# The first residual of two chunks by plain loads and VectorE additions; the sigmoid product and the state copies planned anew

## The chip, the cores and the metric

The kernel runs on one core of a Trainium2 chip. The metric is the device time of one execution in microseconds; several runs are given with their median. The engines are called TensorE (PE in the profile, PEld for its weight loads), VectorE (DVE), ScalarE (ACT), GpSimd (POOL) and SyncE (SP, which here only issues DMAs).

## What is computed

One layer of a hybrid decoder for 1024 prompt tokens and 8 sequences of 4 sample tokens, in f32, with 1024 features:

```python
h = _rmsnorm(x, g_pre_mix[l]) * (1.0 + sc1) + sh1
z = h @ w_in[l]
za, zq, zf, zi, zg, zc = jnp.split(z, split_at, axis=-1)
ya, v_rows = _chunk_gmlp(za, ...)          # gMLP, chunks of 128
yb, S = _hgrn2(zq, zf, zi, zg, ...)        # gated linear recurrence
yc, buf = _conformer_conv(zc, ...)         # depthwise convolution, layer norm, silu
y = jnp.concatenate([ya, yb, yc], axis=-1) @ w_out[l]
x = x + gt1 * _rmsnorm(y, g_post_mix[l])   # first residual
h = _rmsnorm(x, g_pre_mlp[l]) * (1.0 + sc2) + sh2
y = jnp.square(jax.nn.relu(h @ w_up[l])) @ w_down[l]
x = x + gt2 * _rmsnorm(y, g_post_mlp[l])   # second residual
```

`_conformer_conv` ends with `silu(_layernorm(y))`, that is a product of a value and its sigmoid. `_hgrn2` needs the recurrent state at the start of each block of tokens.

## The kernel before

Features lie on the partitions. The 1056 tokens are cut into three chunks (`NCH`) of 352 (`CW`); the sample tokens are the last 32 of chunk 2. A tile of 1024 features by 352 tokens is 8 slices of 128 features; where it is kept in three tiles (`KK`), these hold 3, 3 and 2 slices, that is 1056, 1056 and 704 elements per partition. Each f32 product is made of three matmuls of rounded high and low parts, so each weight block of 128 by 1024 is split after its load: a cast on ScalarE (`whi`), a subtraction on VectorE (`wlo`). `fetch` (line 304) issues the loads on SyncE's queue into three buffers (`raw`), `weights` (line 344) keeps a small stock of split blocks ready.

**Order.** The program is written in the order in which each engine shall run it. A main program issues the matmuls; all else is done by generators in queues (line 216), which `step` (line 224) lets go on between the pieces of a product, as far as the credits of the engines allow. A generator can wait for planned times: `until` (line 244) yields until the class `Plan` (line 39) holds the given tiles for done. `Plan` knows for each engine when it will be free, by formulas for the price of every instruction: on ScalarE 0.1 us and 0.83 ns per element and 1.3 us for a change of table, for a DMA on GpSimd's queue 0.9 us and 8.0 us until it has landed. These times set only the order in which instructions are issued; on the chip semaphores do the waiting, and each engine takes its instructions in the order issued.

**Mixer.** `ORDER` names the blocks of the input projection: two for the convolution, four pairs of the recurrence with their gates, and the gMLP. A product's result stands in one of three PSUM banks (`pm_tile`) until it is evacuated; for a gate that takes a sigmoid on ScalarE (`sgg`) and a product on VectorE (`gq`). `conv_tail` (line 931) normalises the convolution's output and ends, for both halves j, with an affine step in place and a sigmoid on ScalarE and their product on VectorE, issued one behind the other. `recur` (line 1197) makes the recurrence of one pair of heads: the states S, one per block of 64 tokens, are copied by two ScalarE instructions, with dimensions swapped, into `sv[0]` (the tile `vt`, in the profile under the name vf) and `sv[1]` (in `KE`, in the profile K); `until(vt, KE, k2, QE, banks=2)` stands ahead of the matmuls `ob`, which read them.

**Out-projection and first residual.** The y tiles of the mixer are split into `yh` and `yl` by `split_y` for each chunk. For each of the chunks 0, 1, 2 eight blocks m of the output projection follow (line 1519 on); ScalarE evacuates each into `o` and its square for a sum (`tot`). Blocks 6 and 7 keep their split weights for all chunks (the tiles whome). Behind the last block a generator `after_mix` (line 1495) is queued: the root mean square from `tot` (`stps`, `rstd`), the scaling of `o` on VectorE, three DMAs on GpSimd's queue that add x from memory onto `o`, three more that write the sum to memory as `x1d` for the second residual, then squares (ScalarE), their fold (VectorE), a matmul of ones (`stps<-sq`), and the normalisation and modulation in place, which gives the high and low parts of h2 (`h20hi`, `h20lo` for chunk 0 and so on).

**MLP.** TensorE then makes four up-projections for chunk 0, four for chunk 1, eight blocks of down-projection for both, and the same for chunk 2; each first waits, in the program, until that chunk's h2 has been issued. Twelve further rounds follow, in which TensorE has hardly a gap.

The tiles tagged "e" (line 186 on) share 17 buffers (`N_E`): the y tiles, `o` of chunks 0 and 1, the kept weights, later the activations of the MLP. `load3` (line 609) takes three such tiles and loads a chunk of x into them on SyncE's queue.

Of the kernel before, what the change touches and what calls it, by code (L numbers as in the profile page):

```python
# [11 lines left out]
ALU = mybir.AluOpType  # L12
# [14 lines left out]
T_GROUP = 3.57  # L27
# [11 lines left out]
class Plan:  # L39
# [10 lines left out]
    def given(self, key, price, out, ins, extra=0.15):  # L50
        names = [x.tensor.name for x in ins]
        end = max(self.free[key], self.now(), *(self.done.get(x, 0.0) for x in names)) + price
        self.free[key] = end
        out = out.tensor.name
        self.done[out] = end + extra
        for x in (out, *names):
            self.used[x] = max(self.used.get(x, 0.0), end)
        self.moved |= key == "pe"

    def idle(self, t):  # L60

        if not self.moved:
            self.free["pe"] += t
        self.moved = False
# [95 lines left out]
def trunk_kernel(ctx: ExitStack, tc: tile.TileContext, xT, cT, wada0, wada, vec, cst, msk, win, wout, wup,  # L160
# [4 lines left out]
    plan = Plan()  # L165
    PE = Metered(nc.tensor, pe_price, credit, "pe", plan)
    ACT = Metered(nc.scalar, ActPrice(), credit, "act", plan)
    DVE = Metered(nc.vector, dve_price, credit, "dve", plan)
    POOL = Metered(nc.gpsimd, pool_price, credit, "pool", plan)
# [34 lines left out]
    def e3(name):  # L204
        return ep.tile([128, 3, CW], F32, tag="e", name=name)
# [15 lines left out]
    def add_task(kind, gen):  # L221
        queues[kind].append(gen)

    def step(t):

        plan.idle(t)
        t += max(0.0, clock[1] - credit["pe"])
        clock[0] += t
        for k in ("dve", "act", "pool"):
            credit[k] = min(credit[k] + t, t + 0.5)  # L230
        credit["pe"] = clock[1] = min(credit["pe"] + t, 1.0)
        again = True
        while again:
            again = False
            for kind, q in queues.items():
                if q and due[kind] <= clock[0] and all(credit[k] > 0 for k in uses.get(kind, ("dve", "act", "pe"))):
                    try:
                        due[kind] = clock[0] + (next(q[0]) or 0.0)
                    except StopIteration:
                        q.pop(0)  # L240
                    again = True
                    break

    def until(*aps, banks=0):

        while not plan.ready(aps, banks):
            yield 0.2
# [23 lines left out]
    def vc(o, n):  # L271
        return vec_t[:, o:o + n]
# [259 lines left out]
    def add_last(tot):  # L532
        DVE.tensor_tensor(out=tot, in0=tot, in1=pending.pop(), op=ALU.add)
# [72 lines left out]
    def hc(name):  # L606
        return hp.tile([128, 8, CW], F32, tag="c", name=name)

    def load3(src, name):
        ts = []  # L610
        for kk, (k0, n) in enumerate(KK):
            t = e3(f"{name}{kk}")
            SP.dma_start(out=t[:, 0:n, :], in_=src[:, k0:k0 + n, :])
            ts.append(t)
        return lambda kk: ts[kk][:, 0:KK[kk][1], :]
# [233 lines left out]
    ysp = [None] * NCH  # L849

    def split_y(c):
        hi, lo = hc(f"yh{c}"), hc(f"yl{c}")
        for k in Y_ORDER:
            while y_done[k] <= c:
                yield 0.5
            y = ch(ys[k], c)
            ACT.copy(out=r(hi[:, k, :]), in_=y)
            DVE.tensor_tensor(out=r(lo[:, k, :]), in0=y, in1=hi[:, k, :], op=ALU.subtract)
            yield
        ysp[c] = lambda k: (hi[:, k, :], lo[:, k, :])  # L860
# [70 lines left out]
    def conv_tail():  # L931
        while not room(3):
            yield 2.0
        sq, hi, lo = [e("y6")], e("cvhi"), e("cvlo")
        for c in range(NCH):
            DVE.tensor_tensor(out=ch(sq[0], c), in0=ch(cva[0], c), in1=ch(cva[1], c), op=ALU.add)
        yield 4.0

        def halves():
            ACT.copy(out=r(hi), in_=sq[0])  # L940
            POOL.tensor_tensor(out=r(lo), in0=sq[0], in1=hi, op=ALU.subtract)

        halves()
        yield from until(hi, lo)
        for c in range(NCH):
            yield from until(banks=1)
            mu = pb.tile([128, CW], F32, tag="b", name="cmu")
            mean_of(mu, mean256, ch(hi, c), ch(lo, c))
            s2 = rs("sq2")[:, 0:CW]
            for j in range(2):  # L950
                DVE.tensor_tensor(out=ch(cva[j], c), in0=ch(cva[j], c), in1=mu, op=ALU.subtract)
                ACT.activation(out=s2 if j else ch(sq[0], c), in_=ch(cva[j], c), func=AF.Square)
            DVE.tensor_tensor(out=ch(sq[0], c), in0=ch(sq[0], c), in1=s2, op=ALU.add)
            yield
        yield 4.0
        halves()
        yield from until(hi, lo, banks=3)
        vv = [pb.tile([128, CW], F32, tag="b", name="cvv") for c in range(NCH)]
        for c in range(NCH):
            mean_of(vv[c], mean256, ch(hi, c), ch(lo, c))  # L960
        drop(2)
        sq.append(e("y7"))
        for c in range(NCH):
            ACT.activation(out=ch(sq[0], c), in_=vv[c], func=AF.Sqrt, bias=eps, scale=1.0)
        yield 2.0
        for c in range(NCH):
            sd = ch(sq[0], c)
            DVE.reciprocal(out=sd, in_=sd)
            yield
            for j in range(2):  # L970
                a = ch(cva[j], c)
                DVE.tensor_tensor(out=a, in0=a, in1=sd, op=ALU.mult)
            yield
        yield 2.0
        for j in range(2):
            z = cva[j]
            ACT.activation(out=z, in_=z, func=AF.Identity, scale=vc(V_LNG + j, 1), bias=vc(V_LNB + j, 1))
            yield
            ACT.activation(out=sq[j], in_=z, func=AF.Sigmoid)
            DVE.tensor_tensor(out=sq[j], in0=sq[j], in1=z, op=ALU.mult)  # L980
            ys[6 + j] = sq[j]
            y_done[6 + j] = NCH
            drop()
            yield
# [212 lines left out]
    def recur(p, st):  # L1197
# [59 lines left out]
        sv = vt, by_block(KE)  # L1257
# [3 lines left out]
        for i in range(2):  # L1261
# [5 lines left out]
                 in_=D64.rearrange("p (o b) -> p o b", o=1).to_broadcast([128, 32, 16]))  # L1267
# [4 lines left out]
        for hh in range(2):  # L1272
            o = 64 * hh
            ACT.copy(out=sv[hh][o:o + 64, 1:16], in_=S[o:o + 64, :, 0:15].rearrange("p d b -> p b d"))
        ACT.copy(out=hg_o[:, p, :], in_=S[:, :, 15])

        yield from until(vt, KE, k2, QE, banks=2)
# [10 lines left out]
        oo, sq, hi, lo = k2, vf, e("gnhi"), e("gnlo")  # L1288
# [19 lines left out]
        for hh in range(2):  # L1308
# [7 lines left out]
                           op=ALU.mult)  # L1316
# [175 lines left out]
    def extra(name):  # L1492
        return e2.tile([128, 3, CW], F32, tag="e2", name=name)

    def after_mix(c, src, tot):
        box = []
        yield 1.0
        yield from until(tot, banks=1)
        rstd = rstd_of(tot)
        yield  # L1500
        for kk in (normed(c, src, rstd, Go1) if c == 2 else scaled(c, src, rstd, ())):
            k0, n = KK[kk]
            POOL.dma_start(out=src(kk), in_=xT[c][:, k0:k0 + n, :], accum_op=ALU.add)
            yield
        for kk, (k0, n) in enumerate(KK):
            POOL.dma_start(out=x1d[c, :, k0:k0 + n, :], in_=src(kk))
        yield from until(*(src(kk) for kk in range(3)))
        for d in sum_squares(src, box):
            yield d
        hi, lo = hc(f"h2{c}hi"), hc(f"h2{c}lo")  # L1510
        for d in modulated(c, src, box.pop(), G2, sh2, hi, lo):
            yield d
        h2[c] = (hi, lo)
# [5 lines left out]
    for c in range(NCH):  # L1519
        src, o = blocks_of([(e3 if c < 2 else extra)(f"o{c}") for kk in KK])  # L1520
        tot = w2.tile([128, CW], F32, tag="tot", name="tot", bufs=2)
        while ysp[c] is None:
            step(T_GROUP / 2)
        for m in range(8):
            w = w_kept[m] if m in w_kept else weights()
            if m in KEPT:
                w_kept[m] = w
            ps = pm_tile()
            product8(ps, w, ysp[c], Y_ORDER)
            if c == 2 and m in (2, 3, 4, 5, 6):  # L1530
                split_next()
            if c < 2:
                ACT.activation(out=o(m), in_=ps, func=AF.Identity, scale=Go1[:, m, 0:1])
            else:
                ACT.copy(out=o(m), in_=ps)
            add_square(tot, ps, m, DVE)
            step(T_GROUP / STEPS)
            if c == 0 and m in (1, 3):
                add_task("first", split_y(1 + m // 2))
        add_last(tot)  # L1540
        add_task(("recur", "turn", "stage")[c], after_mix(c, src, tot))


    acc = [None] * NCH
# [423 lines left out]
    acts, more = {}, {}  # L1968
# [12 lines left out]
    for g, parts in enumerate(GROUPS):  # L1981
        tot = tots[:, 2 * g:2 * g + 2, :].rearrange("p a n -> p (a n)")[:, 0:sum(b - a for c, a, b in parts)]
# [113 lines left out]
```

## Time and profile before

| | us |
|---|---|
| runs | 1258.51, 1260.38, 1264.3 |
| median | 1260.38 |
| the profiled execution | 1263.86 |
| its span, first to last instruction | 1262.1 |
| its mean granted clock of TensorE | 0.990 |

The span is what the profile's times count in; the execution's own time has 1.8 us around it. In the profile nearly all instructions bear line 113, the helper that records them, so they are told apart by the names of their tiles: `a<-b,c` is an instruction that writes a and reads b and c. In a group's row stand the instruction, its shape, the count, then the busy time and the mean of one, then the idle time of the engine ahead of it and what ended that. In a row of a timeline stand start, duration, engine, line, operation, and in brackets the engine's idle time ahead of it with what ended it.

### The profile page before, as it was taken

To read this page: it belongs to the slowest core of one execution; us is meant where nothing else is said; L and a number is where in the kernel's file an instruction comes from. 1 tells how busy PE (TensorE), PEld (TensorE's weight loads), DVE (VectorE), ACT (ScalarE), POOL (GpSimd) and SP (SyncE) were. 2 spreads that over 40 slices of the span, in tenths; PEclk is the share of its full clock that TensorE was granted. 3 is DMA by queue.
4 is the path that set the end of the run, shared out by engine and by line. 5 is a ranking of instruction groups with operands and counts; after the bars stand their busy time and mean duration, and the time that the engine had idled before them with its cause. 6 is when DMAs were issued, how large, how long until landed. Compare 5 with 4: busy or idle time off the path is not lost.

```text
span 1262.1 us, 20853 instructions
## 1 busy us (share of the span) xinstructions
PE 1221.9 (97%) x8614; PEld 1171.4 (93%) x8614; DVE 902.0 (71%) x1469; ACT 533.6 (42%) x989; POOL 63.0 (5%) x107
## 2 busy tenths in 40 slices
PE   9999999999899999999999999999999999999995
PEld 7888889999889999899999999999999999999994
DVE  5799889688658768866686657657666765765766
ACT  6513464684854746555423312322331331231533
POOL 1000020211010011000000000000000000000001
PEclk9999999999999999999999999999999999999998
DMA  9458401111111466243201211210211120111218
GB/s 367 170 217 277 168 26 52 43 59 47 35 43 40 151 192 182 85 134 106 79 18 50 68 34 34 68 49 19 68 50 34 51 68 32 36 67 35 108 18 210
DMA packets 48846, 113.22 MB, mean 90 GB/s; under 512 B 10336, under 2 KB 24832, under 8 KB 48624
## 3 DMA queue, kind: packets, MB, share of 16 engines
q1 hardware_dynamic: 44432, 99.22, 22.9%
q0 software_dynamic: 4320, 12.68, 4.3%
q8 instruction: 67, 1.10, 0.4%
q14 instruction: 27, 0.22, 0.1%
HBM read 101.75 MB, written 10.14 MB: 89 GB/s over the span
## 4 chain that ended last, share of the span: by engine, by line
PE 78%; DVE 11%; ACT 6%; DMA 3%; issue 2%; POOL 0%; SPq 0%; DVEq 0%; ACTq 0%
PE pmt L113 71%; DVE acc L113 2%; PE adaps L113 1%; DMA rawada<-in_wada 1%; DVE T L113 1%; PE pmt L744 1%; DVE wlo L113 1%; DMA o<-in_xT 1%; ACT K L113 1%; ACT vf L113 1%; DVE q L113 1%; PE sc L113 1%; DVE rsq L113 1%; ACT relu L113 1%; PE ob L113 1%
## 5 line engine op out<-in xcount | busy, mean ns | idle before, releaser
L113 PE MATMUL pmt<-ah,whi 128*128 128x352 f32 (+2 forms) x744 | 244.0, 328 | 7.9 <-DVE acc L113 5.8
L113 PE MATMUL pmt<-al,whi 128*128 128x352 f32 (+2 forms) x744 | 241.3, 324 | 1.3 <-DVE al L113 1.3
L113 PE MATMUL pmt<-ah,wlo 128*128 128x352 f32 (+2 forms) x744 | 240.1, 323 | 0.0
L113 DVE TENSOR_TENSOR acc<-acc,pmt 128x352 f32<-128x352 f32 (+1 forms) x320 | 158.5, 510 | 91.8 <-PE pmt L113 91.6
L113 DVE TENSOR_TENSOR wlo<-raw,whi 128x1024 fp32r<-128x1024 f32 (+2 forms) x113 | 134.5, 1192 | 46.2 <-ACT whi L113 46.2
L113 ACT CAST whi<-raw 128x1024 fp32r<-128x1024 f32 (+2 forms) x113 | 114.2, 1014 | 107.9 <-PE pmt L113 105.8
L113 PEld LDWEIGHTS pmt<-ah,whi 128*128 128x128 f32 x744 | 139.7, 188 | 15.3 <-DVE acc L113 10.7
L113 PEld LDWEIGHTS pmt<-al,whi 128*128 128x128 f32 x744 | 139.9, 188 | 4.2 <-DVE al L113 2.0
L113 PEld LDWEIGHTS pmt<-ah,wlo 128*128 128x128 f32 x744 | 139.9, 188 | 0.4
L113 ACT COPY acc<-pmt 128x352 f32<-128x352 f32 x63 | 28.4, 452 | 196.7 <-PE pmt L113 161.8
L113 PE MATMUL pmt<-h22hi,wlo 128*128 128x352 f32 x256 | 82.7, 323 | 0.0
L113 PE MATMUL pmt<-h22hi,whi 128*128 128x352 f32 x256 | 82.5, 322 | 0.0
L113 PE MATMUL pmt<-h22lo,whi 128*128 128x352 f32 x256 | 82.3, 322 | 0.0
L113 DVE SCALAR_TENSOR_TENSOR cva<-cvx,vec_t,cva 128x1024 f32<-128x1024 f32 x60 | 77.7, 1295 | 1.2
L113 PE MATMUL pmt<-s,whi 128*128 128x352 f32 x312 | 75.6, 324 | 0.0
L113 ACT ACTIVATE relu<-pmt 128x352 f32<-128x352 f32 x57 | 26.4, 463 | 104.2 <-PE pmt L113 101.3
L113 DVE TENSOR_TENSOR al<-rsq,ah 128x352 fp32r<-128x352 f32 x96 | 49.1, 523 | 15.7 <-ACT ah L113 9.6
L113 PE MATMUL pmt<-h1hi,whi 128*128 128x352 f32 x168 | 55.7, 332 | 2.6 <-DVE gq L113 2.6
L113 PE MATMUL pmt<-h2hi,whi 128*128 128x352 f32 x168 | 56.7, 337 | 0.0
L113 PE MATMUL pmt<-h0hi,whi 128*128 128x352 f32 x168 | 55.5, 330 | 0.8 <-DVE gq L113 0.8
L113 PEld LDWEIGHTS pmt<-s,whi 128*128 128x128 f32 x312 | 54.5, 188 | 0.0
L113 DVE TENSOR_TENSOR rsq<-relu 128x352 f32<-128x352 f32 x45 | 23.5, 523 | 43.0 <-ACT relu L113 41.8
(391 smaller groups left out, 2941.0 us busy)
## 6 DMA issues: line engine op xcount, KB each, us to landing
rawada<-in_wada SPq DMA_DIRECT2D x48, 512.0 KB, 8.3
raw<-in_wup SPq DMA_DIRECT2D x36, 512.0 KB, 3.5
raw<-in_wdn SPq DMA_DIRECT2D x48, 256.0 KB, 3.1
raw<-in_win SPq DMA_DIRECT2D x22, 512.0 KB, 3.6
raw<-in_wout SPq DMA_DIRECT2D x20, 512.0 KB, 3.5
raw<-in_wdn SPq DMA_DIRECT2D x12, 512.0 KB, 3.5
x<-in_xT SPq DMA_DIRECT2D x6, 528.0 KB, 7.0
o<-in_xT POOLq DMA_DIRECT2D x6, 528.0 KB, 7.8
```

The costliest lines, as they stand in the source:

```text
L113: return f(**kw)
L744: nc.tensor.matmul(out=pss[m, c], lhsT=r(w_first[m][i % 2][:, k, :]), rhs=r(h[c][i // 2][:, k, :]), start=k == i == 0, stop=k == 7 and i == 2)
```

## The change

1. `Plan.more` is new: it lengthens the planned work of an engine and the planned end of tiles, without any instruction.
2. In `conv_tail` the affine step counts for 0.9 us more, and the product of sigmoid and value is issued only when the plan holds the sigmoid for done; the second half's activations are issued behind the first half's product.
3. In `recur` each of the two state copies counts for 0.95 us more.
4. For chunks 0 and 1, behind block 6 of the out-projection, x is loaded again into three tiles of SyncE's queue, once the y parts of chunks 1 and 2 have been issued. `after_mix` adds these tiles to `o` on VectorE, straight behind each scaling, in place of the accumulating DMAs.
5. Chunk 2 keeps its accumulating DMAs and gets a pause of 4.0 us of the plan's clock behind the writes of x1.

```diff
+    def more(self, key, t, *outs):
+        self.free[key] += t
+        for x in outs:
+            x = x.tensor.name
+            self.done[x] = max(self.done[x], self.free[key] + 0.15)
+            self.used[x] = max(self.used[x], self.free[key])
...
             ACT.activation(out=z, in_=z, func=AF.Identity, scale=vc(V_LNG + j, 1), bias=vc(V_LNB + j, 1))
+            plan.more("act", 0.9, z)
             yield
             ACT.activation(out=sq[j], in_=z, func=AF.Sigmoid)
+            yield from until(sq[j])
             DVE.tensor_tensor(out=sq[j], in0=sq[j], in1=z, op=ALU.mult)
...
             ACT.copy(out=sv[hh][o:o + 64, 1:16], in_=S[o:o + 64, :, 0:15].rearrange("p d b -> p b d"))
+            plan.more("act", 0.95, sv[hh])
...
-    def after_mix(c, src, tot):
+    def after_mix(c, src, tot, x):
...
-            POOL.dma_start(out=src(kk), in_=xT[c][:, k0:k0 + n, :], accum_op=ALU.add)
+            if x:
+                DVE.tensor_tensor(out=src(kk), in0=src(kk), in1=x(kk), op=ALU.add)
+            else:
+                POOL.dma_start(out=src(kk), in_=xT[c][:, k0:k0 + n, :], accum_op=ALU.add)
             yield
         for kk, (k0, n) in enumerate(KK):
             POOL.dma_start(out=x1d[c, :, k0:k0 + n, :], in_=src(kk))
+        if not x:
+            yield 4.0
...
+        x_again = None
...
+            if c < 2 and m == 6:
+                while not (ysp[1] and ysp[2]):
+                    step(T_GROUP / 2)
+                x_again = load3(xT[c], f"xa{c}_")
         add_last(tot)
-        add_task(("recur", "turn", "stage")[c], after_mix(c, src, tot))
+        add_task(("recur", "turn", "stage")[c], after_mix(c, src, tot, x_again))
```

## The prediction

> **What bounds the kernel now.** I read the page first, then who waited for whom on TensorE, then TensorE's timeline at the longest of these waits, then stretches of 3.4 us around them.
>
> ```profile
> span 1262.1 us, 20853 instructions
> PE 1221.9 (97%) x8614; PEld 1171.4 (93%) x8614; DVE 902.0 (71%) x1469; ACT 533.6 (42%) x989; POOL 63.0 (5%) x107
> PE 78%; DVE 11%; ACT 6%; DMA 3%; issue 2%; POOL 0%; SPq 0%; DVEq 0%; ACTq 0%
> ```
>
> TensorE is busy for 1221.9 of 1262.1 us. The change takes no matmul away, so it can only win from the 40.2 us in which TensorE is idle and from time at a lower clock. Which of these gaps does it touch? The waits of TensorE name them:
>
> ```profile
> PE pmt L113 <- DVE gq L113: 3.5, 2, 2.6
> PE ob L113 <- ACT K L113: 3.2, 4, 1.5
> PE pmt L113 <- DVE h21lo L113: 2.4, 1, 2.4
> PE stps L113 <- DVE sq L113: 2.2, 1, 2.2
> PE ob L113 <- ACT vf L113: 0.5, 1, 0.5
> 329.68 0.43 PE L113 MATMUL pmt<-h1hi,whi 128*128 128x352 f32 x1 [2.63 <-DVE gq L113]
> 354.50 0.27 PE L113 MATMUL ob<-QB,K 128*64 128x64 f32 x1 [1.52 <-ACT K L113]
> 468.22 1.54 PE L113 MATMUL stps<-sq,cst_t 128*128 128x352 f32 x2 [2.22 <-DVE sq L113]
> 527.90 0.43 PE L113 MATMUL pmt<-h21lo,whi 128*128 128x352 f32 x1 [2.39 <-DVE h21lo L113]
> ```
>
> The first rows are total, count, longest; the last four are start, duration, and in brackets the idle time before. `stps<-sq` is the sum of squares after chunk 0's first residual, `h21lo` the end of the same work for chunk 1, `ob<-QB,K` the matmuls that need the copied states, and `gq` a gate product that stands on VectorE behind the sigmoid products. Three of the four gaps leave a second loss behind (columns: stretch, length, busy us of PE, PEld, DVE, ACT, POOL with counts, granted clock, DMA share, GB/s):
>
> ```profile
> 328.00:331.40 3.40, 1.72 (x11) 1.72 (x12) 3.40 (x7) 3.32 (x8) 0.00 (x0) 1.00 0.00 0
> 331.40:334.80 3.40, 2.94 (x47) 2.62 (x47) 3.29 (x5) 3.31 (x8) 0.00 (x0) 1.00 0.34 107
> 351.90:355.30 3.40, 1.35 (x32) 1.08 (x34) 1.63 (x4) 3.35 (x5) 0.00 (x0) 1.00 0.00 0
> 355.30:358.70 3.40, 3.40 (x44) 3.28 (x40) 0.00 (x0) 3.19 (x7) 1.46 (x2) 0.50 0.00 0
> 464.60:468.00 3.40, 1.40 (x9) 1.11 (x7) 3.30 (x5) 0.91 (x2) 0.00 (x0) 0.99 0.69 242
> 468.00:471.40 3.40, 3.18 (x9) 2.68 (x10) 2.14 (x4) 0.55 (x1) 0.00 (x0) 0.50 0.00 0
> 526.00:529.40 3.40, 1.50 (x9) 1.47 (x10) 2.57 (x4) 1.61 (x4) 0.00 (x0) 1.00 0.15 60
> 529.40:532.80 3.40, 3.40 (x14) 3.40 (x13) 3.33 (x7) 0.97 (x3) 0.00 (x0) 0.50 0.02 5
> ```
>
> Where TensorE was busy for 1.35, 1.40 or 1.50 us of a stretch, the next 3.4 us were granted half the clock; after 1.72 us busy they were not. Half the clock over 3.40 us costs some 1.7 us (1.6 where 3.18 us were busy).
>
> **Chunks 0 and 1 of the first residual.** Each loses three accumulating DMAs from GpSimd's queue and gains three plain loads on SyncE's queue and three additions on VectorE. What stood between the last scaled block and the last square before:
>
> ```profile
> 447.30 2.06 DVE L113 TENSOR_TENSOR o<-o,rstd 128x1056 f32<-128x1056 f32 x2
> 461.17 0.79 ACT L113 ACTIVATE sq<-o 128x704 f32<-128x704 f32 x1 [1.93 <-DMA o<-in_xT]
> 489.51 2.05 DVE L113 TENSOR_TENSOR o<-o,rstd 128x1056 f32<-128x1056 f32 x2
> 503.55 0.79 ACT L113 ACTIVATE sq<-o 128x704 f32<-128x704 f32 x1 [1.83 <-DMA o<-in_xT]
> o<-in_xT POOLq DMA_DIRECT2D x3, 352.0 KB, 11.3
> 325.65 1.26 DVE L113 TENSOR_TENSOR y<-y,cva 128x1056 f32<-128x1056 f32 x1 [3.29 <-ACT y L113]
> ```
>
> For chunk 0 scaling ended at 449.36 and the last square began at 461.17: 11.8 us, nearly all of it the last DMA's 11.3 us to landing. Chunk 1: 491.56 to 503.55, 12.0 us. An addition of two full tiles of 1056 is the row of 1.26 us; two of these and one of 704 elements (two thirds, estimated 0.9) make 3.4 us per chunk, 6.8 in all. So the two chains get 8.4 and 8.6 us shorter. Two weight subtractions of 1.2 us may come between (VectorE does one per weight block, the row of 436.55 below), which leaves about 6 us. TensorE waited for 2.22 and 2.39 us, so both waits should go, with some 3.5 us to spare: **3.8 us** (2.2 + 1.6) and **4.1 us** (2.4 + 1.7).
>
> The 6.8 us on VectorE cost nothing as long as its next user isn't late: weights are split ahead of use (cover below), and VectorE is busy for 71% overall. If that cover is gone, each chunk's chain still gives back only 3.4 of the 8.4 us. Late next is the write of x1, whose source the normalisation overwrites in place:
>
> ```profile
> x1d<-o POOLq DMA_DIRECT2D x2, 528.0 KB, 8.6
> 464.87 3.30 DVE L113 TENSOR_TENSOR sq<-sq 128x1056 f32<-128x1056 f32 x4
> 442.60 2.35 DVE L113 RECIPROCAL rstd<-rstd 128x352 f32<-128x352 f32 x1 [0.94 <-ACT rstd L113]
> ```
>
> It lands 8.6 us after its issue. Between the addition and the overwriting stand three squares (0.79 for the smaller, by size an estimated 1.2 for each larger), the fold (3.30), the matmul (1.54) and the reciprocal (2.35), together some 10 us; so it is not late, by little.
>
> **The loads' place on SyncE's queue.** They stand behind the weight loads issued up to block 6 of the chunk and ahead of those after it.
>
> ```profile
> x<-in_xT SPq DMA_DIRECT2D x6, 528.0 KB, 7.0
> raw<-in_wout SPq DMA_DIRECT2D x20, 512.0 KB, 3.5
> 436.55 1.23 DVE L113 TENSOR_TENSOR wlo<-raw,whi 128x1024 fp32r<-128x1024 f32 x1 [2.19 <-ACT whi L113]
> 447.61 1.05 ACT L113 CAST whi<-raw 128x1024 fp32r<-128x1024 f32 x1
> 407.42 33.96 PE pmt L113 x210
> ```
>
> There are three raw buffers: the one freed at 437.78 is cast again at 447.61, 9.8 us later, and a load takes 3.5, so 6.3 us are spare. Three loads of x (1408 KB) at the weights' rate of 512 KB in 3.5 us take 9.6 us; the nearest rows of such loads say 7.0 each, when many run at once. The weight behind them would be cast up to 3.3 us late, and two prepared weights cover 7.7 (24 matmuls each, and by the row of the chain 210 take 33.96 us, so 3.9 us per weight). The x tiles are asked for ahead of the weight that takes the buffer freed at 437.78, and the second one is wanted from 447.30 on, where its block is scaled: 9.5 us. Cost taken **0**, bounds 0 and the price in rival 3.
>
> The tiles that the loads land in held the y blocks, whose copies for chunk 2 the loop makes sure are planned before the load is issued; the added waiting there has nothing behind it but the next weight load.
>
> **State copies.** Nothing is added or removed on the engines; the planner's price rises.
>
> ```profile
> L113 ACT COPY vf<-q 64x960 f32<-64x960 f32 x4 | 7.6, 1905 | 12.8 <-DVE q L113 12.8
> L113 ACT COPY K<-q 64x960 f32<-64x960 f32 x4 | 7.4, 1844 | 0.1
> ```
>
> By its formula (0.1 + 960 x 0.83 ns) the planner held each for 0.90 us; they take 1.9 and 1.84, and the added 0.95 makes it 1.85. So `ob` is issued 1.9 us later per pair, with matmuls of the input projection in its place. The waits to be won are 3.2 + 0.5 = 3.7 us and the half clock at 355.3, 1.7: 5.4 at most. The last of them (1.52 and 0.53 at one place) is slightly longer than 1.9, and what is queued behind `ob` (the norms and VectorE's work on them) moves back by the same 1.9 us, with gate and gMLP blocks as cover. Bounds 0 and 5.4; I take **4.4**.
>
> **Sigmoid product.** VectorE now gets the product only when the planner holds the sigmoid for done.
>
> ```profile
> 323.23 1.27 ACT L113 ACTIVATE cva<-cva,vec_t 128x1056 f32<-128x1056 f32 x1
> 326.82 1.08 ACT L113 ACTIVATE y<-cva 128x1056 f32<-128x1056 f32 x1
> 327.92 0.82 ACT L113 ACTIVATE sgg<-pmt 128x352 f32<-128x352 f32 x2
> 329.11 0.52 DVE L113 TENSOR_TENSOR gq<-pmt,sgg 128x352 f32<-128x352 f32 x1
> ```
>
> VectorE stood for 3.29 us before the first product (the row of 325.65), and the gate product that frees TensorE's bank came at 329.11, behind both. But ScalarE is late too: the gate's own sigmoid ran only at 327.92, after both pairs of activations (323.23 to 327.90). The gain comes only if the second pair now goes behind it. Bounds 0 and 2.6; I take half, **1.3**.
>
> **Chunk 2's pause of 4.0 us** costs nothing: no wait of TensorE names that chunk's h2 (h22), so other matmuls cover it now, and the whole chain behind TensorE's work for chunk 1 moves forward with that; without the cover it would cost at most its 4.0.
>
> **A new order.** Every changed price reorders all that is issued behind it, from the first pair on. The trace can't show the waits of an order that doesn't exist; the bounds are a gain of one wait like the present ones and a loss of one with its half clock (2.4 + 1.7 = 4.1). I take **1.6** as a loss.
>
> **The sum.** 3.8 + 4.1 + 4.4 + 1.3 - 1.6 = 12.0 us. The profiled execution took 1263.9 (span 1262.1 and 1.8 around it): 1251.9. The median of the runs shown is 1260.4, 3.5 below it, which is two half-clock windows of 1.7; if a usual run lacks two of the three windows, its gain is 12.0 - 3.4 = 8.6. So the median lies between 1248.4 and 1251.8: **1250.0**.
>
> What does the clock rule make of it? Two stalls of 2.22 and 2.39 us were each followed by a clock of 0.50, as shown. The Trainium skill, "TensorE: Matmul & The Clock Gate", section "HAM oscillation — how this bites in real kernels", warns only of idle gaps above some 3.4 us, by which none of these gaps would cost clock; here the trace disagrees, and the measurement decides.
>
> **Rivals.**
>
> 1. *The plan's edits give nothing*: ScalarE's queue stays late, the waits for `ob` and `gq` come back elsewhere. For it: the gate's sigmoid at 327.92. Then 3.8 + 4.1 less the loss of 1.6 to 4.1 remains, 3.8 to 6.3: 1254.1 to 1256.6. Chance 0.18.
> 2. *The change doesn't do what it says for chunk 1*: the DMA goes, but VectorE's queue (weight subtractions, sums, chunk 0's work) spends the 6 us and `h21lo` stays last. For it: VectorE was busy 2.57 of 3.40 us before that wait. Then 4.1 less, and half of the plan's gain with the same reordering loss: 3.8 + 2.2 + 0.6 - 1.6 = 5.0, less clock that a usual run lacks: 1255 to 1259. Chance 0.08.
> 3. *Slower*: the x loads starve the weights. If they run one after another at 7.0 each, 21 us, a weight is 21 + 3.5 - 9.8 = 14.7 us late, 7.0 beyond the cover of 7.7, and TensorE drops to half clock: 8.7 per chunk, 17.4 for two, against 12.0 won: 1265.8, and up to 1268 with less won. It decides from 14 us for three loads on. Against it: a weight load of the same size takes 3.5. Chance 0.05.
> 4. *Only idle time is won*: the half-clock windows don't go, because other stretches with under 1.6 us of work appear or because a usual run has none. The 2.63 us gap of 329.68 cost no clock, being spread over two stretches. Then 2.2 + 2.4 + 2.7 + 1.3 - 1.6 = 7.0: 1253.4. Chance 0.07. (By the rule of the Trainium skill's "TensorE: Matmul & The Clock Gate" the time would come out here.)
>
> The forecast, 1246 to 1253, has 0.58; more than it, up to the ceiling of 3.8 + 4.1 + 5.4 + 2.6 = 15.9 (1244.5), 0.04. The range is 1244.5 to 1259: below it nothing is left to win, above it stands rival 3 with what goes wrong beside it. Half a per cent, 6.3 us, is about what a measurement of this kernel can tell from no change: faster means below 1254.1. Forecast, the better case and rival 4 make 0.69, less a little for its upper edge: 0.68. Rivals 1 and 2 make the same, 0.26, with the edge 0.27. Slower: 0.05.
>
> **What would show it.** Residual: no wait of `stps<-sq` and `h21lo` on TensorE, no 0.50 clock behind them, additions `o<-o,xa` of 1.26 us straight after the scalings, squares some 6 us earlier. Loads: the first addition not waiting for `xa`. Copies: `ob<-QB,K` without its waits, clock 1.00 after it. Sigmoid: VectorE's wait for y under 1 us, the gate product before 327. Wrong it would be if weights (`whi<-raw`) wait for their DMA, if TensorE shows new waits of over 4 us in all between 150 and 600, or if the clock drops at new places.

## The result, and the profile after

| | median us | runs | ratio to before (95%) |
|---|---|---|---|
| before | 1260.58 | 1258.51 to 1264.3 | |
| changed | 1270.97 | 1269.75 to 1271.66 | 1.0078 (1.0053 to 1.0103) |

The changed kernel is slower by 0.8%, 10 us, where 1250.0 with a range of 1244.5 to 1259.0 was forecast. Its profiled execution took 1271.1 us. The page of the changed kernel begins so (span, busy time by engine, engines of the chain that ended last):

```profile
span 1269.3 us, 20856 instructions
PE 1220.1 (96%) x8614; PEld 1170.3 (92%) x8614; DVE 911.5 (72%) x1475; ACT 535.9 (42%) x992; POOL 61.4 (5%) x101
PE 76%; DVE 14%; ACT 7%; issue 2%; DMA 0%; POOL 0%; SPq 0%; DVEq 0%; ACTq 0%
```

The DMA has gone from the chain (3% to 0%), as the additions should make it; VectorE has taken its share and more (11% to 14%). Of the list of who waited for whom on TensorE (total, times, longest) these rows tell what went and what came; those of the later MLP rounds and of the span's two ends are left out:

```profile
PE pmt L121 <- DVE h21lo L121: 3.0, 2, 2.8
PE cvv L121 <- ACT K L121: 2.8, 1, 2.8
PE gmsp L121 <- DVE gmt L121: 2.7, 1, 2.7
PE pmt L121 <- DVE yl L121: 2.4, 2, 1.3
PE cvv L121 <- DVE QB L121: 2.1, 1, 2.1
PE pmt L121 <- ACT vf L121: 1.9, 2, 1.3
PE pmt L121 <- DVE q L121: 1.8, 1, 1.8
PE pmt L121 <- DVE gq L121: 1.6, 1, 1.6
PE stps L121 <- DVE sq L121: 1.1, 1, 1.1
```

The waits of `ob` for the state copies are gone, and so is that of chunk 0's sum of squares (the 1.1 us left belong to chunk 2, near 551). The wait for `h21lo` stayed and grew. Six of the rows shown are new (or were 0.2 us: `cvv` for QB), all in the mixer or at the out-projection's start: `cvv`, the variance of the convolution's output, twice, `gmsp` of the gMLP, and a projection's product `pmt` that waits for `yl` (a y tile's low part), `vf` or `q`. Stretches of both kernels, first before, then after (length, busy us of PE, PEld, DVE, ACT, POOL, granted clock, DMA share, GB/s):

```profile
120.00:570.00 450.00, 437.02 (x3622) 414.91 (x3622) 344.33 (x490) 263.11 (x487) 50.70 (x77) 0.99 0.28 90
240.00:300.00 60.00, 59.42 (x587) 57.94 (x586) 46.19 (x64) 38.82 (x68) 7.53 (x17) 1.00 0.10 32
```

```profile
120.00:570.00 450.00, 430.15 (x3575) 408.26 (x3574) 351.70 (x492) 262.52 (x485) 49.10 (x71) 0.98 0.27 89
240.00:300.00 60.00, 51.87 (x473) 49.92 (x472) 43.02 (x63) 34.18 (x69) 12.16 (x17) 0.94 0.11 36
```

From 120 to 570 TensorE stood for 13.0 us before and 19.9 after. The stretch 240 to 300 alone went from 0.6 to 8.1 us. At the three longest gaps, behind 284, 411 and 526, stretches of 3.4 us read in the changed kernel:

```profile
284.00:287.40 3.40, 1.01 (x4) 0.64 (x4) 0.53 (x1) 3.25 (x9) 2.98 (x2) 0.99 0.31 125
287.40:290.80 3.40, 1.33 (x6) 1.14 (x5) 2.65 (x4) 2.82 (x5) 1.32 (x2) 0.50 0.00 0
290.80:294.20 3.40, 3.40 (x13) 3.40 (x12) 3.24 (x7) 1.72 (x3) 1.25 (x3) 0.50 0.00 0
413.70:417.10 3.40, 1.50 (x8) 0.92 (x6) 3.29 (x9) 1.82 (x3) 0.00 (x0) 1.00 0.00 0
417.10:420.50 3.40, 2.85 (x10) 2.82 (x11) 2.64 (x8) 1.23 (x2) 0.00 (x0) 0.50 0.00 0
526.30:529.70 3.40, 0.58 (x4) 0.34 (x3) 2.64 (x4) 2.50 (x5) 0.00 (x0) 1.00 0.03 10
529.70:533.10 3.40, 3.09 (x10) 2.26 (x9) 3.40 (x8) 1.58 (x3) 0.00 (x0) 0.50 0.48 154
533.10:536.50 3.40, 3.40 (x12) 3.22 (x12) 3.24 (x8) 1.08 (x2) 0.00 (x0) 0.50 0.00 0
```

Five of them have half the clock: two in a row behind the first gap, one behind the second, two behind the third. Taken as half the busy time, it costs an estimated (1.33 + 3.40 + 2.85 + 3.09 + 3.40) / 2 = 7.0 us, against (3.40 + 3.18 + 3.40) / 2 = 5.0 in the three such stretches before. With the idle time that is 6.9 + 2.0 = 8.9 us, near the 7.2 by which the spans differ.

**How the largest gap arises.** Rows of GpSimd, ScalarE and TensorE near 280, before and then after. `cvlo` is the low part that `cvv` multiplies, `sc` the scores of pair 2.

```profile
276.45 2.44 POOL L113 TENSOR_TENSOR cvlo<-y,cvhi 128x1056 fp32r<-128x1056 f32 x1 [34.34 <-ACT cvhi L113]
277.62 0.22 PE L113 MATMUL scs<-q,k 64*32 64x32 f32 x2
280.81 0.32 PE L113 MATMUL cvv<-cvhi,means 128*128 128x352 f32 x1
```

```profile
282.23 1.08 ACT L121 ACTIVATE k<-f 128x1056 f32<-128x1056 f32 x1
283.21 0.22 PE L121 MATMUL scs<-q,k 64*32 64x32 f32 x2
283.22 1.05 ACT L121 CAST cvhi<-y 128x1056 fp32r<-128x1056 f32 x1
284.36 2.41 POOL L121 TENSOR_TENSOR cvlo<-y,cvhi 128x1056 fp32r<-128x1056 f32 x1 [0.48 <-ACT cvhi L121]
286.34 0.43 PE L121 MATMUL cvv<-cvhi,means 128*128 128x352 f32 x1 [2.85 <-ACT K L121]
289.69 0.63 PE L121 MATMUL cvv<-cvhi,means 128*128 128x352 f32 x1 [2.07 <-DVE QB L121]
```

Before, `cvlo` was ready at 278.9, and `cvv` came at 280.8 with projection matmuls between the scores and it. After, `cvv` stands right behind the scores, and TensorE waits twice. By the code the scores, the transposed keys (`ktps`) and the three tiles of `cvv` share five PSUM banks. The first wait ends, by the brackets, with ScalarE's last copy of `K` out of such a bank (286.29), the second with the masked copy of the scores into `QB` (289.55), which frees the bank for `cvv`'s third tile. `cvlo`, whose cast stood behind pair 3's activations on ScalarE, was ready only at 286.77, half a microsecond behind the first of these. The price itself adds no instruction: the pieces have been dealt out in another order. What the order adds is table loads on ScalarE, 1.28 us each: 22 in the changed kernel, 19 before.

### The profile page after: what moved, and what is told of

The parts are those of the page before. It is cut to its first block, busy times and chain, and to the rows that moved or that the text cites. A ratio compares the mean times of both kernels' runs of the same rounds, so it can differ in the third digit from the quotient of the medians.

```text
span 1269.3 us, 20856 instructions
## 1 busy us (share of the span) xinstructions
PE 1220.1 (96%) x8614; PEld 1170.3 (92%) x8614; DVE 911.5 (72%) x1475; ACT 535.9 (42%) x992; POOL 61.4 (5%) x101
## 4 chain that ended last, share of the span: by engine, by line
PE 76%; DVE 14%; ACT 7%; issue 2%; DMA 0%; POOL 0%; SPq 0%; DVEq 0%; ACTq 0%
PE pmt L121 69%; DVE acc L121 2%; PE adaps L121 1%; PE stps L121 1%; DVE T L121 1%; DVE wlo L121 1%; DVE vf L121 1%; PE pmt L752 1%; ACT vf L121 1%; PE sc L121 1%; DVE o L121 1%; ACT whi L121 1%; PE us L121 1%; ACT K L121 1%; DVE rsq L121 1%
## 5 line engine op out<-in xcount | busy, mean ns | idle before, releaser
L121 PE MATMUL pmt<-h1hi,wlo 128*128 128x352 f32 x168 | 54.7, 325 | 0.0
L121 PE MATMUL pmt<-h1lo,whi 128*128 128x352 f32 x168 | 54.6, 325 | 0.0
```

Source lines behind the costliest of these rows:

```text
L121: return f(**kw)
```

## Experiments

Every kernel is the one before with the edits named. The letters in the expectations: A, the two edits of the plan lose the time, the state copies most of it, and the residual part trades one wait for another; B, the residual part loses it (additions on VectorE, loads of x); C, the sigmoid product loses it; D, the first pair's `ob` misses one turn of the plan and that sets the loss; E, the loss grows in proportion to the added price; F, chunk 2's statistics overtake chunk 1's normalisation; G, H, P and Q are told in their own texts.

### One part at a time

state_only has the first of these edits, sig_only the next two, sig_state all three of them, res_only the residual part (the loads, the additions, the pause for chunk 2).

```diff
+            plan.more("act", 0.95, sv[hh])
...
+            plan.more("act", 0.9, z)
...
+            yield from until(sq[j])
...
+                DVE.tensor_tensor(out=src(kk), in0=src(kk), in1=x(kk), op=ALU.add)
...
+                x_again = load3(xT[c], f"xa{c}_")
```

> Only the residual part: x loaded again for chunks 0 and 1, additions on VectorE, pause for chunk 2; both plan edits undone. Theory A (the plan edits lose the time by moving the recurrence back; the residual part has swapped one wait for another): 1254 to 1260 us, no new wait of TensorE ahead of 410 us, the wait for chunk 0's squares gone, a wait for h21lo still there or gone. Theory B (the residual part loses the time, through VectorE's additions and the loads): 1265 to 1270 us, the waits all behind 440 us.

> Only the sigmoid part: 0.9 us more for the affine step and the product held back until the plan has the sigmoid done. Theory A: 1257 to 1261 us, the gate product's wait of 2.6 us shorter or gone, all ahead of 310 us as before. Theory C (the held product keeps tiles and VectorE's order so that pair 3 is late): 1264 to 1270 us, pair 3's scores after 345 us.

> Only the 0.95 us per state copy in the plan; no instruction is added or taken away. Theory A: 1264 to 1270 us, the matmuls ob come 2 to 6 us later behind us in each pair, pair 3's scores some 20 us later than 333.9, waits of cvv (convolution variance) and at the start of the out-projection. Theory B: 1255 to 1260 us, the waits of ob gone and nothing in their place. Theory C (the sigmoid product loses it): as theory B.

> Both plan edits without the residual part. Theory A: 1268 to 1275 us, that is the changed kernel's waits ahead of 420 us and the waits for chunk 0's squares and h21lo of the kernel before. Theory B: under 1258 us.

| | median us | ratio (95%) |
|---|---|---|
| res_only | 1261.51 | 1.0005 (0.9995 to 1.0014) |
| sig_only | 1263.73 | 1.0019 (1.0009 to 1.0028) |
| state_only | 1270.11 | 1.0069 (1.0051 to 1.0086) |
| sig_state | 1269.34 | 1.0062 (1.0044 to 1.0081) |

The state copies' price, which adds no instruction of its own, makes nearly the whole loss; the residual part gains nothing and loses nothing. So A holds for the cause, and B and C fall as that. A's times for res_only (1254 to 1260) and sig_only (1257 to 1261) were missed by 1.5 and 2.7 us, both to the slow side. Alone, the sigmoid's edits lose 2 to 3 us, in the way that C had named, though less: the 2.63 us wait for `gq` goes, but pair 3's states come late (rows of sig_only: VectorE's reciprocals of a norm, the scan behind them, ScalarE's copy, TensorE):

```profile
344.73 4.57 DVE L121 RECIPROCAL vf<-vf 128x352 f32<-128x352 f32 x2
350.90 2.32 DVE L121 TENSOR_TENSOR_SCAN q<-decs,q 128x512 f32<-128x512 f32 x2
353.31 1.81 ACT L121 COPY vf<-q 64x960 f32<-64x960 f32 x1 [8.10 <-DVE q L121]
355.17 0.48 PE L121 MATMUL ob<-k,vf 128*64 128x64 f32 x2 [5.31 <-ACT vf L121]
```

Beside the state copies they cost nothing that shows: sig_state and state_only differ by less than their intervals.

### The size of the price, and which pair pays

The first line is state_070; state_085 has 0.85 in its place. The other two are state_first; state_rest has p > 0.

```diff
+            plan.more("act", 0.70, sv[hh])
...
+            if p == 0:
+                plan.more("act", 0.95, sv[hh])
```

> The state copies alone, with 0.70 us each in place of 0.95: the plan then holds the second copy of the first pair for done just ahead of a poll instead of just behind it. Theory D (the loss comes from one missed poll: the next thing in the queues, an ada step of 1.9 us of TensorE and more, goes first, and the pairs' chain moves back by some 5 us at each pair and 22 at the last): ob of the first pair at 165 instead of 170 us, pair 3's scores before 340, waits of ob nearly gone, 1254 to 1260 us. Theory E (any later issue of ob is paid for in proportion): three quarters of the loss, 1266 to 1268 us, pair 3's scores near 350.

> The same with 0.85 us each, 0.15 more than state_070 and 0.10 less than the change. Theory D: the poll is missed, so the time jumps to 1266 to 1272 us, ob of the first pair at 170. Theory E: 0.15 us more per copy, at most 2 us slower than state_070.

> The kernel before with the longer price (0.95) on the state copies of the first pair alone; pairs 1 to 3 keep the old price. Theory P (the loss is made once, at the first pair: its ob misses one turn of the plan, and every later piece of the mixer, the convolution's tail with them, is dealt out in another order): 1266 to 1271, with pair 3's ob near 375 to 379 of the span, the wait of the gMLP matmul gmsp for gmt near 411 and a half-clock window next to it. Theory Q (each pair's later issue adds its share): a quarter of the loss, 1261 to 1264, and no wait at 411.

> The kernel before with the longer price (0.95) on the state copies of pairs 1, 2 and 3; the first pair keeps the old price. P: the first pair's ob is issued where it was (163.7), so nothing of the loss, 1252 to 1261, pair 3's ob before 360. Q: three quarters of the loss, 1266 to 1269.

| | median us | ratio (95%) | first `ob` of pair 0 |
|---|---|---|---|
| state_070 | 1251.47 | 0.9931 (0.9912 to 0.995) | 164.1 |
| state_085 | 1256.57 | 0.9967 (0.9957 to 0.9978) | 169.6 |
| 0.95 (state_only) | 1270.11 | 1.0069 (1.0051 to 1.0086) | 170.0 |
| state_first | 1265.36 | 1.0043 (1.0027 to 1.0058) | 168.8 |
| state_rest | 1252.96 | 0.994 (0.9927 to 0.9954) | 162.9 |

The first of four matmul forms, as the view of the tile `ob` gives it (shortest, median, longest ns, first and last start), of before, state_first and state_rest:

```profile
L113 PE MATMUL ob<-k,vf x128: 218/222/316, 163.7 to 356.8; 128*64 128x64 f32 x120, 64*64 64x64 f32 x8
```

```profile
L121 PE MATMUL ob<-k,vf x128: 218/222/270, 168.8 to 372.4; 128*64 128x64 f32 x120, 64*64 64x64 f32 x8
```

```profile
L121 PE MATMUL ob<-k,vf x128: 218/222/270, 162.9 to 354.5; 128*64 128x64 f32 x120, 64*64 64x64 f32 x8
```

With 0.70 the stretch from 120 to 570 reads

```profile
120.00:570.00 450.00, 443.44 (x3702) 422.84 (x3702) 350.52 (x499) 269.72 (x501) 51.85 (x77) 1.00 0.30 92
```

TensorE stands for 6.6 us there, against 13.0 before, no matmul `ob` waits, and no stretch has half the clock. This execution still waits 2.08 us for chunk 0's squares and 2.38 for `h21lo`, with the full clock behind both; the last section comes back to that.

0.95 on the first pair alone costs 5 us, 0.95 on the other three alone wins 7.4: E and Q fall, since a loss in proportion would have three quarters of itself in the last kernel. P holds in its sign and misses in its size: state_first came out at 1265.4, under its 1266 to 1271, and the wait of `gmsp` near 411 is not in it, while the two of `cvv` near 286 are (4.40 and 1.63 us). What happens at the first pair is seen in the copy and the first `ob` of before and of the changed kernel:

```profile
163.02 1.87 ACT L113 COPY K<-q 64x960 f32<-64x960 f32 x1
163.73 0.27 PE L113 MATMUL ob<-k,vf 64*64 64x64 f32 x1
```

```profile
162.57 1.93 ACT L121 COPY K<-q 64x960 f32<-64x960 f32 x1
169.40 0.27 PE L121 MATMUL ob<-k,vf 64*64 64x64 f32 x1
```

The copies end at 164.9 and 164.5. Before, `ob` begins while the second copy still runs (its first matmuls need none); after, it stands 4.9 us behind the copies' end. By the code, the generator can ask the plan only when `step` gives it a turn; a turn at which the plan still holds the copies for running is lost, and here the next one put `ob` 5.7 us later. From there on the credits fall otherwise, and what was dealt out from 240 on differs. D is half right: the turn is missed at 0.85 too, which is still faster than before. D's times were missed on both sides (1254 to 1260 for 0.70, 1266 to 1272 for 0.85), and so were E's.

The effects don't add: +5.0 and -7.4 us alone, +9.6 together.

### What the residual part lacks

res_hold2 is the residual part with the first edit, which holds chunk 2's statistics; state_070_res_hold2 is the same with 0.70 per state copy; state_070_res0 has 0.70 and the residual part for chunk 0 alone (the second edit; chunk 1, which keeps its DMAs, then gets the pause of 4.0 too); state_070_sig 0.70 and the sigmoid's two edits.

```diff
+        while c == 2 and h2[1] is None:
+            yield 0.5
...
-            if c < 2 and m == 6:
+            if c in (0,) and m == 6:
```

> The residual part alone, and chunk 2's statistics held back until chunk 1's h2 is issued. Theory F (in the residual part chunk 2's reciprocal and scaling, 4.5 us of VectorE, overtake chunk 1's normalisation, and that keeps the wait for h21lo): that wait and its half clock go, 1253 to 1257 us, chunk 1's high parts from 510 us. Theory G (VectorE is simply full there, the 6.8 us of additions): the wait stays at 2 us or more, 1259 to 1262 us.

> Both of the above together. Theories D and F: the gains add up, 1248 to 1254 us. If D falls: 1258 to 1264 us.

> 0.70 per state copy and the change's residual for chunk 0 only; chunk 1 keeps the accumulating DMAs. If chunk 0's wait (2.08 at 457.74 with 0.70) simply goes and chunk 1's comes no earlier: 1247 to 1250, the wait of stps for sq near 458 gone, that of pmt for h21lo at 2 to 3 us. If VectorE's additions for chunk 0 only push the wait to the up-projection as in the residual part alone: 1251 to 1253.

> 0.70 per state copy and both edits of the sigmoid product (0.9 more for the affine, the product held until the sigmoid is due). If the product's edits are worth their own wait where the order is kept: 1249 to 1251. If they make VectorE's reciprocals late for pair 3's scan as they did alone: 1253 to 1256, with a wait of ob for vf of over 3 us near 350.

| | median us | ratio (95%) |
|---|---|---|
| res_hold2 | 1261.59 | 1.001 (1.0 to 1.0019) |
| state_070_res_hold2 | 1251.59 | 0.993 (0.9915 to 0.9945) |
| state_070_res0 | 1249.37 | 0.9911 (0.9898 to 0.9924) |
| state_070_sig | 1255.09 | 0.9962 (0.9949 to 0.9975) |

Holding chunk 2 back wins nothing, so F falls; the times are G's, whose reason (VectorE is full) is tested below. Chunk 0's residual wins some 2 us by the medians beside 0.70 (1251.47), but the two intervals overlap, so this gain is not shown clear of noise. The two chunks together, with chunk 2 held, win none. The sigmoid's edits cost 3.6 us here too, though by another wait than expected: none of `ob` near 350, but `yl` (1.79) at 400 and half the clock behind the residual's waits. In res_only, the additions of chunk 1 and what follows read:

```profile
492.56 0.89 DVE L113 TENSOR_TENSOR o<-o,xa 128x704 f32<-128x704 f32 x1
498.18 2.74 ACT L113 ACTIVATE sq<-o 128x1056 f32<-128x1056 f32 x3
505.31 2.35 DVE L113 RECIPROCAL rstd<-rstd 128x352 f32<-128x352 f32 x1
509.80 2.35 DVE L113 RECIPROCAL rstd<-rstd 128x352 f32<-128x352 f32 x1
519.77 0.43 PE L113 MATMUL pmt<-h21lo,whi 128*128 128x352 f32 x1 [2.72 <-DVE h21lo L113]
```

The last addition ends at 493.45, the squares begin at 498.18. With DMAs the last of them began at 503.55: of the 8.6 us that the chain was to be shorter, 4.7 are gone by the squares' place in ScalarE's queue. The first reciprocal is chunk 2's, the second chunk 1's; with chunk 2 held back, chunk 1's blocks stand between the evacuations of chunk 0's up-projection, and the waits stay (1.95 us for `h21hi` at 520.6, 2.89 for `h21lo` at 523.9). By the code, the squares are late because `until` holds them until the plan has the additions for done, and their next turn comes behind other pieces. To test that, they were issued at once, and left to the semaphore:

```diff
-        yield from until(*(src(kk) for kk in range(3)))
+        if c == 2:
+            yield from until(*(src(kk) for kk in range(3)))
         for d in sum_squares(src, box):
```

(Chunk 2's pause is left out in these.)

> The residual part alone (additions for chunks 0 and 1, the pauses of 4.0 gone), and the squares of chunks 0 and 1 issued right behind the additions instead of when the plan's clock has the additions done. Theory H (the shorter chain is given back in the plan: its squares are issued in the same place of ScalarE's queue as before, behind evacuations of the out-projection, so an earlier sum wins nothing): with the squares early the statistics of chunk 1 come 3 to 6 us earlier and both waits go, 1253 to 1258. Rival (VectorE's 3.4 us of additions per chunk and the loads are what holds the normalisation): no gain over the residual part alone, 1260 to 1263, and pmt waits for h21lo or h21hi as before.

> 0.70 per state copy and the residual part with the squares of chunks 0 and 1 issued right behind the additions. H: both waits gone, 1244 to 1249. Rival: 1251 to 1253, as with the squares held back.

> As the last one, and chunk 2's statistics held until chunk 1's h2 is issued. H: as the last one or up to 2 us less, 1243 to 1249, if chunk 2's reciprocal (2.35) still stood ahead of chunk 1's. Rival: 1251 to 1253.

| | median us | ratio (95%) |
|---|---|---|
| res_now | 1255.32 | 0.9964 (0.9953 to 0.9975) |
| state_070_res_now | 1247.76 | 0.9904 (0.9888 to 0.9919) |
| state_070_res_now_hold2 | 1247.76 | 0.99 (0.9882 to 0.9917) |

Rows of res_now:

```profile
492.13 0.89 DVE L113 TENSOR_TENSOR o<-o,xa 128x704 f32<-128x704 f32 x1
492.67 2.74 ACT L113 ACTIVATE sq<-o 128x1056 f32<-128x1056 f32 x3
502.82 2.35 DVE L113 RECIPROCAL rstd<-rstd 128x352 f32<-128x352 f32 x1 [1.73 <-ACT rstd L113]
520.53 0.43 PE L113 MATMUL pmt<-h21hi,whi 128*128 128x352 f32 x1 [1.52 <-ACT h21hi L113]
```

The additions end within 0.5 us of where they did, the squares begin 5.5 us earlier, chunk 1's reciprocal 7 us earlier, the wait for `h21lo` is gone but for 0.2 us, and the kernel is 6.2 us faster than res_only by the medians, 5.2 by the ratios to before of their own rounds. Beside 0.70 and with chunk 2 held in both, the same step wins 3.8 us (1251.59 to 1247.76). The pause of chunk 2 is left out in the same step; by the program it stands behind chunk 2's scaling, which in res_only ran at 507.95, so it can't have moved chunk 1's squares, but whether it has a share in the time was not tried. H holds, with one miss: not both waits go, 1.5 us for `h21hi` and one stretch at half the clock stay, since chunk 1's last blocks are still issued between chunk 0's evacuations. The rival (VectorE's additions and the loads) falls, and G with it: res_now makes the same additions and loads.

The last two kernels beat both given ones, by 1.0% and 1.8%: 1247.76 us. Their page (state_070_res_now) and its stretch from 120 to 570:

```profile
span 1247.2 us, 20854 instructions
PE 1214.1 (97%) x8614; PEld 1165.6 (93%) x8614; DVE 907.8 (73%) x1475; ACT 532.7 (43%) x989; POOL 58.7 (5%) x101
```

```profile
120.00:570.00 450.00, 446.19 (x3712) 425.72 (x3711) 358.46 (x508) 270.27 (x501) 46.47 (x71) 1.00 0.29 93
```

3.8 us of idle time are left there, of 13.0.

## Why the prediction was wrong, step by step

**State copies: the step that failed.** "So `ob` is issued 1.9 us later per pair, with matmuls of the input projection in its place", with a gain between 0 and 5.4. The waits of `ob` went as forecast, but the first pair's `ob` was 5.7 us later, not 1.9, because the plan is asked only at its turns. It isn't the 5.7 us themselves that cost, since other matmuls stood there: TensorE was busy for 119.87 us of the 120 from 120 to 240, and for 51.87 of the 60 behind them. The term was taken at +4.4 and measured at -9.6 (state_only); with 0.70 in place of 0.95 it was +9.3, above the upper end too. So both ends were wrong. The missed turn alone doesn't set the sign either: 0.85 missed it and won 4.2 us. What failed is the step from one later matmul to its own cover, with the order of all later pieces left as it was.

**A new order.** A loss of 1.6, at most 4.1 (one wait and its half clock). The six new rows add up to 13.7 us (2.8 + 2.7 + 2.4 + 2.1 + 1.9 + 1.8), with three stretches at half clock. An order that differs from the first pair on is not one wait's risk: every later piece is dealt anew, and several can land badly. The text on "what would show it" had named this, new waits of over 4 us between 150 and 600, but the bound had not been drawn from it.

**Chunk 0's residual**, 3.8: right in its mechanism, not shown in its size. The wait of 2.22 us and the half clock at 468 are gone in the changed kernel; beside 0.70 it measured 2.1 us (1251.47 to 1249.37), with intervals that overlap, and there the wait (2.08) had no half clock behind it that could be won.

**Chunk 1's residual**, 4.1: wrong as changed. The step "so both waits should go, with some 3.5 us to spare" counted what engines must do between addition and `h21lo`, with two weight subtractions, and not where the squares and the normalisation stand in the order issued. In the changed kernel the same 4.7 us are lost: squares at 507.77, while the third addition ended at 503.04. Issued at once they win 6.2 us over res_only by the medians, without the pause. Rival 2 had the outcome for chunk 1, with VectorE's queue as its reason; the runs show ScalarE's queue and the plan's turn.

**VectorE's 6.8 us and the loads at nothing**: right. The six loads landed in 4.5 to 7.1 us, no addition waited for one, and res_now has all of them and gains. Rival 3 did not come about.

**Sigmoid**, +1.3 (0 to 2.6): measured alone as a loss of 3.2 us by the medians, and of 3.6 beside 0.70. In sig_only the wait of 2.63 us for `gq` went as said; pair 3's scan or, beside 0.70, a y tile came late instead. Again an end of the bound, nothing lost, was taken for certain without a reason.

**Chunk 2's pause**, at nothing: not tried by itself, so open. TensorE waits 1.1 us for chunk 2's sum of squares in the changed kernel and in res_only, which both have the pause, and not in the kernel before or in res_now, which have none; but neither does it in res_hold2, which has it.

**Rival 1**, waits that come back elsewhere, was the nearest by its mechanism; it kept the residual's gain and one wait's loss, and so stopped at 1256.6.

**What stays open.** Missing the first pair's turn gave 1265.4 with the other pairs at the old price, 1256.6 with 0.85 for all, 1270.1 with 0.95 for all. Which of the pieces between the first pair and 240 carries that was not settled; that `cvv` stands directly behind pair 2's scores is seen in the trace and wasn't undone alone. One thing parts the kernels that lose by this price from the others: in the changed one, state_only, sig_state and state_first the last sigmoid of the convolution's tail begins on ScalarE at 348.7 to 349.7, among pair 3's copies (22 or 23 table loads in all, four of them around the tail's last steps in the changed kernel). Before it begins at 326.8 and with 0.85 at 325.0, ahead of most of these copies, with 19 loads in both. From 300 to 420 TensorE stands for 7.4 us in the changed kernel, 6.0 in the one before and 0.05 with 0.85. No run moved the tail alone, so that this is the cause is not shown.

## What to carry to other kernels

A planner's price is no local edit: ask at which of its turns the piece will be issued, and price the re-dealt order behind it from a scan of values (0.70, 0.85 and 0.95 here gave 1251.5, 1256.6 and 1270.1), before any one value is kept because it matches a measured duration. When a transfer is replaced by a faster step, check that the piece behind it is also issued earlier; where a semaphore waits anyway, issuing it at once was worth 3.8 to 6.2 us here, with a pause of chunk 2 left out beside it.

## What was not expected of the hardware

Half the clock can last for two stretches in a row, even where the first of them was busy: after 0.58 us busy in 526.30 to 529.70, both following ones had 0.50, the first with 3.09 of 3.40 us busy; in the kernel before, after 1.40 us busy, one such stretch with 3.18 busy was followed by the full clock. Nor is the half clock a fixed price of a wait. The same wait of 2.63 us for `gq` at 329.68 had the full clock behind it in the profile of the kernel before, and 0.50 from 331.0 to 334.0 in that of res_only; in state_070 waits of 2.08 and 2.38 us had none. Three terms of the prediction hold 1.6 or 1.7 us of clock each, seen in one execution; its median and rival 4 allowed for runs that lack them. The runs don't show what decides it. No single wait before the changed kernel's stretches was longer than 2.85 us; the Trainium skill, "TensorE: Matmul & The Clock Gate", section "HAM oscillation — how this bites in real kernels", warns of idle gaps above some 3.4 us, and here the trace disagrees, as it did before the change.
